# Up projection: eight column pairs with two feature blocks by seven products instead of four, and their quarters loaded by GpSimd

## The chip, the core and the metric

The kernel runs on one core of a Trainium2 chip. A core has a matrix engine (TensorE, PE in the profile; its weight loads are PEld), three engines for other arithmetic (VectorE or DVE, ScalarE or ACT, GpSimd or POOL), and SyncE (SP), which here only issues loads and stores. Each engine runs its own list of instructions in order and waits for others by semaphores. Loads move between the chip's memory and the core's SBUF; TensorE writes into PSUM, eight banks of 128 x 512 float32. The metric is the device time in microseconds, lower is better. Three runs of the kernel before gave a median of 1549.39 us (1548.16 to 1551.18).

## The reference

One decoder layer over 256 tokens of width 2048, all in float32: a norm, a combined input projection, two parallel token mixers, an output projection, a residual sum, then the part that matters here and a final norm:

```python
h = rmsnorm(x, norm_ffn_w[l])
gate, up = jnp.split(jnp.einsum('bsd,df->bsf', h, w_up[l]), 2, axis=-1)
gate = causal_dwconv(gate, conv_ffn_w[l]) + conv_ffn_b[l]
x = x + jnp.einsum('bsf,fd->bsd', jax.nn.gelu(gate, approximate=False) * up, w_down[l])
```

The up projection multiplies the 256 x 2048 activations by a 2048 x 11264 weight matrix: 5632 gate columns and 5632 up columns.

## The kernel before

**Precision and tiles.** Weights come as tiles of 256 x 512 (`raw`, 512 KB a load). ScalarE rounds a tile to float32r (`whi`, L278), VectorE subtracts that from the tile (`wlo`, L286), and a product is three matmuls: high by high, low activation by high weight, high activation by low weight. `whi` and `wlo` have three buffers each and `raw` four; `weights()` makes tiles two ahead of the one in use.

**Stages.** Input projection and mixers come first, then the output projection (L321 to L323, from `w_out`), the up projection (L1353, 819 to 1303 us of the span), and the down projection (L1338).

**The up projection** goes by 11 column pairs c = 0 to 10, each 512 gate columns and the 512 up columns that belong to them. The 2048 features are four blocks of 512. A block is either done plainly, by four steps `("plain", c, col, kp)` of 12 matmuls (two 256-feature halves by gate and up; `up_plain`), or as a 2 x 2 block product by seven products instead of eight (Strassen and Winograd's form): feature halves j, token halves t, gate and up as the two columns. `chunks_of[c]` says which blocks go by seven: none in pair 0, block 0 in every other pair, and blocks 1 and 0 in the pairs of `TWO`, (1, 3, 5, 7).

**The seven products** (`up_product`, L1356 and on) are T1, 11, T2, 21, T3, 22, T4, with 6 matmuls each. 11, 21 and 22 use one quarter of the weights as it is, and T1 to T4 use sums of quarters, which `up_sum` (L219) makes on VectorE in place: four a block. Four quarters of a block are loaded by `quad_load` (L213) with SyncE into homes (`UP_HOMES`), buffers that hold something else earlier or later: xt0 to xt3 for block 0, hhi8 to hlo9 for block 1. The activations' sums (`ups`) are made once, in pair 0, for blocks 0 and 1 alike.

**Banks.** T1 opens an own bank (from the pool `psm`, two buffers, which the transposed gate and up use as well) and ends in a copy to SBUF (L1382). 11 opens the bank of gate and second token half; behind the last block's 11, ScalarE copies that bank to the gate's other token half (L1386), and T2, T3 and T4 go on adding into the first one. Before the first 21 and behind the last T3, VectorE adds the own bank to make the two banks of up (L1375, L1389).

**The order around them** is written out by hand in `up_steps` and fixed for TensorE. With g a plain gate step, u a plain up step of pair c, and p a product of pair c + 1, the last up steps of c (`rest`) are put between the first products of c + 1. Before a pair of `TWO` six up steps are kept back (`tail`): T1, u, 11, u (block 1), T1, u, 11, u (block 0), T2, u (block 1), T2, u (block 0), then 21 twice, the transposes of pair c's gate (L1415), T3 twice, 22 twice, the transposes of its up, T4 twice. The gate's convolution (L1305, L1310), gelu, and the product with up follow during the next plain steps. `when` says how many steps ahead of its place each quarter's load is written. The order on ScalarE, VectorE, GpSimd and the queues is a scheduler's, made when the program is built.

**GpSimd** before loads only the down projection's quarters (L232) and some small things; the second norm's power (L560) runs on it at 824.63 us.

Of the kernel before, what the change touches and what calls it, by code (L numbers as in the profile page):

```python
# [8 lines left out]
F32 = mybir.dt.float32  # L9
# [5 lines left out]
P = 128  # L15
# [20 lines left out]
def kernel(  # L36
# [20 lines left out]
    nc = tc.nc  # L57
# [11 lines left out]
    def nm(s):  # L69
        cnt[0] += 1  # L70
        return f"{s}_{cnt[0]}"
# [5 lines left out]
    def cols(w, base, nk):  # L77
        return [w[c * 256 : (c + 1) * 256, base : base + 512].rearrange("(k p) f -> p k f", p=P)
                for c in range(nk // 2)]
# [13 lines left out]

    srcs += outw[0][:6] + outw[1][:6] + outw[0][6:] + outw[1][6:] + outw[2] + outw[3]
    NUP = DFF // 512
    TWO = (1, 3, 5, 7)
    chunks_of = [()] + [(1, 0) if c in TWO else (0,) for c in range(1, NUP)]
    UP_PARTS = ("T1", "11", "T2", "21", "T3", "22", "T4")
    up_w = [(cols(w_up[0], 512 * c, KD), cols(w_up[0], DFF + 512 * c, KD)) for c in range(NUP)]
    up_steps = []  # L100
    TAIL = 3
    for c in range(NUP):
        kps = [kp for kp in range(KD // 2) if kp // 2 not in chunks_of[c]]
        gate_steps, up_only = ([("plain", c, col, kp) for kp in kps] for col in range(2))
        tail = 6 if c + 1 in TWO else TAIL
        up_steps += gate_steps[:tail]
        for a, b in zip(gate_steps[tail:], up_only):
            up_steps += [a, b]
        rest = up_only[-tail:]
        if c + 1 == NUP:  # L110
            up_steps += rest
            break
        parts = [[("part", c + 1, what, ch) for what in UP_PARTS] for ch in chunks_of[c + 1]]
        up_steps += [("loads", c + 1)]
        if c + 1 in TWO:
            first_four = [parts[ch][n] for ch in range(2) for n in (0, 1)] + [parts[ch][2] for ch in range(2)]
            for a, b in zip(first_four, rest):
                up_steps += [a, b]
            p21, t3, p22, t4 = ([parts[ch][n] for ch in range(2)] for n in range(3, 7))
            up_steps += p21 + [("gate", c)] + t3 + p22 + [("up", c)] + t4  # L120
        else:
            t1, p11, t2, p21, t3, p22, t4 = parts[0]
            up_steps += [t1, rest[0], p11, rest[1], t2, rest[2], p21, ("gate", c), t3, p22, ("up", c), t4]
# [5 lines left out]
    sums_behind = {}  # L129
    for n, src in enumerate(srcs):  # L130
        if isinstance(src, tuple):
            what, ch = src[2:]
            if src[1] not in TWO:
                behind = {"T1": [(n, "T2", 0)], "T2": [(n, "T3", 0), (n, "T4", 0)]}.get(what, [])
            else:
                behind = {("11", 1): [(n, "T1", 0), (n + 1, "T2", 1)], ("T1", 0): [(n + 1, "T2", 0)],
                          ("T2", 1): [(n, "T3", 1), (n + 1, "T4", 1)],
                          ("T2", 0): [(n, "T3", 0), (n + 1, "T4", 0)]}.get((what, ch), [])
            for at_, sum_, of in behind:
                sums_behind.setdefault(at_, []).append((sum_, of))  # L140
    down = [cols(w_down[0], 512 * c, KF) for c in range(4)]

    SEVEN = (8, 9, 10)
# [36 lines left out]
    made = []  # L180
# [3 lines left out]
    last_load = [None]  # L184
# [19 lines left out]
    up_quarters = {}  # L204
    UP_BUFFER = {"11": 0, "T1": 1, "T2": 1, "T3": 0, "21": 2, "22": 3, "T4": 1}

    UP_HOMES = (("xt0", "xt1", "xt2", "xt3"), ("hhi8", "hlo8", "hhi9", "hlo9"))

    def quad_load(c, n):

        ch, i = n // 4, (1, 0, 3, 2)[n % 4]
        up_quarters[ch, i] = fp.tile([P, 2, 512], F32, tag=UP_HOMES[ch][i], name=nm("quad"))
        last_load[0] = nc.sync.dma_start(up_quarters[ch, i], up_w[c][i % 2][2 * ch + i // 2]).ins  # L213

    def up_sum(what, ch):
        b11, b12, b21, b22 = (up_quarters.get((ch, i)) for i in range(4))
        for out_, plus_, minus_ in {"T1": [(b12, b12, b11)], "T2": [(b12, b22, b12)],
                                    "T3": [(b11, b12, b11)], "T4": [(b12, b21, b12)]}[what]:
            nc.vector.tensor_tensor(out_, plus_, minus_, op=ALU.subtract)  # L219
# [15 lines left out]
    def quarter(half, chunk, what, ch=0):  # L235

        if half == "up":
            return up_quarters[ch, UP_BUFFER[what]]
        b11, b12, b21, b22 = (quarters.get((half, chunk, w)) for w in ("11", "12", "21", "22"))
        sums = {"T1": (b11, b12, b11), "T3": (b12, b22, b12), "T2": (b22, b22, b11), "T4": (b21, b21, b22)}  # L240
        return sums[what] if what in sums else quarters[half, chunk, what]
# [24 lines left out]
    def begin(n):  # L266
        while len(made) < min(len(srcs), n):
            load(len(made) + 1)
            raw = loads[len(made)]
            if isinstance(raw, tuple):  # L270
                raw, plus, minus = raw
                nc.vector.tensor_tensor(raw, plus, minus, op=ALU.subtract)
            src = srcs[len(made)]
            shape = list(raw.shape)
            keep = kept.get(len(made))
            hi = wpool.tile(shape, F32R, tag="whi", name=nm("whi")) if keep is None else \
                mtile(keep, shape, F32R, nm("khi"))
            nc.scalar.copy(hi, raw)  # L278
            if shape[1] == 8:
                lo = None  # L280
                nc.vector.tensor_tensor(hi[:, :, 32:64], raw[:, :, 0:32], hi[:, :, 0:32].bitcast(F32),
                                        op=ALU.subtract)
            else:
                lo = wpool.tile(shape, F32R, tag="wlo", name=nm("wlo")) if keep is None else \
                    mtile(4 + keep, shape, F32R, nm("klo"))
                last_split[0] = nc.vector.tensor_tensor(lo, raw, hi.bitcast(F32), op=ALU.subtract).ins  # L286
                splits.append(last_split[0])
            made.append((hi, lo))
            for what, ch in sums_behind.get(len(made) - 1, ()):
                up_sum(what, ch)  # L290
            if isinstance(src, tuple) and src[0] != "up" and src[2] in ("T1", "T3", "T2", "T4"):
                next_quarter()

# [93 lines left out]
    def mtile(i, shape, dt, name):  # L387
        return big.tile(shape, dt, tag=f"m{i}", name=name)
# [280 lines left out]
    tail = mp.tile([P, NH], F32, name="tail")  # L669
# [538 lines left out]
    fp = ctx.enter_context(tc.tile_pool(name="ffn", bufs=1))  # L1208
# [217 lines left out]
    for i, step in enumerate(up_steps):  # L1426
        if step[0] == "part":
            up_product(*step[1:])
            if step[2] == "T4" and step[3] == chunks_of[step[1]][-1]:
                def elementwise(c=step[1] - 1, gates=gates, ups=ups):  # L1430
                    yield from gate_part(c, gates)
                    up_part(c, ups)
                    yield

                work[:] = [elementwise()]
        elif step[0] == "gate":
            gates = turned_pair(pending[step[1], 0])
        elif step[0] == "up":
            ups = turned_pair(pending[step[1], 1])
        elif step[0] == "plain":  # L1440
            up_plain(*step[1:])
            if step[1:] == (0, 0, 1):
                turned_rows()
            if step[1] == 0 and step[2] == 0 and step[3] in (3, 5):
                up_ups.append(up_sums(len(up_ups)))
            if step[1] == NUP - 1 and step[2] == 0:
                if step[3] == 5:
                    half_sums(SEVEN[0])
                if 4 <= step[3]:
                    next_quarter()  # L1450
            if work:
                next(work[0], None)
        for n, step in enumerate(up_steps):
            if step[0] == "loads":
                when = (6, 5, 4, 3, 12, 11, 10, 9) if step[1] in TWO else (8, 7, 6, 5)
                for q in sorted(range(len(when)), key=lambda q: -when[q]):
                    if max(n - when[q], 0) == i:
                        quad_load(step[1], q)
                if n - 3 == i:
                    up_sum("T1", chunks_of[step[1]][0])  # L1460
    pe_order.close()

    xts = {}
# [32 lines left out]
    for hf in range(2):  # L1496
# [11 lines left out]
        for n, step in enumerate(steps[hf]):  # L1508
# [9 lines left out]
            if step[0] == "plain":  # L1518
                kp, c = step[1], step[2] % 2
                more = any(x[0] == "plain" and x[2] % 2 == c for x in steps[hf][n + 1 :]) or hf == 1  # L1520
# [4 lines left out]
            chunk, what = step[1:]  # L1525
# [128 lines left out]
```

## Time and profile before

| | us |
|---|---|
| median of three runs | 1549.39 |
| the profiled execution | 1548.64 |
| its span, first to last instruction | 1546.8 |
| TensorE busy | 1533.0 |
| VectorE busy | 1227.4 |
| ScalarE busy | 842.9 |
| GpSimd busy | 65.6 |

A line of a group names the source line, the engine, the operation, what it writes and reads, its shape and its count; behind the bar stand the busy time, the mean of one in ns, and the engine's idle time just before, with what ended it. A line of a window gives its length, then the busy time and count of each engine, the granted clock, the DMA engines' busy share and GB/s. A line of the chain gives start, length and what ran. A line of the timeline gives start, length and the instruction, with its engine's idle time in brackets where it waited. A line of waits gives who waited for whom, the total, the count and the longest.

### The profile page before, as it was taken

The page shows a single profiled execution, that of the slowest core. Times are in us where ns is not written, and L with a number is a line of the kernel's source. Part 1 is how long each engine was busy: PE and PEld are TensorE (multiplying, and loading weights), DVE is VectorE, ACT ScalarE, POOL GpSimd, SP SyncE. Part 2 cuts the span into 40 slices and gives each one's busy share as a digit, 9 for nine tenths or more (in the row PEclk, how much of TensorE's full clock was granted, in tenths as well). Part 3 has the DMA queues.
Part 4 walks back from the last instruction along what each step waited for, and adds up shares of the span by engine and source line. Part 5 has one row for each costly group of instructions (what it writes and reads, how often), then busy time and mean ns, then how long its engine had stood idle before and what let it go on. Part 6 is the DMA issues. An engine that isn't in the chain of part 4 may idle for free.

```text
span 1546.8 us, 20166 instructions
## 1 busy us (share of the span) xinstructions
PE 1533.0 (99%) x7326; PEld 1264.2 (82%) x7326; DVE 1227.4 (79%) x1748; ACT 842.9 (54%) x1051; POOL 65.6 (4%) x82
## 2 busy tenths in 40 slices
PE   9999999999999999999999999999999999999998
PEld 8888888788888888888877888888888888788886
DVE  6688858896689858887585898888888876878885
ACT  6455446454545445454454666666666665545552
POOL 1010002000100000000000000000000000000100
PEclk9999999999999999999999999999999999999999
DMA  8776757776577756675686565757656667556652
GB/s 276 210 224 206 202 155 224 210 215 181 166 236 210 199 168 200 215 211 183 211 305 191 180 206 163 218 171 220 178 175 192 190 199 256 189 186 204 222 191 90
DMA packets 167698, 310.46 MB, mean 201 GB/s; under 512 B 19459, under 2 KB 23331, under 8 KB 167471
## 3 DMA queue, kind: packets, MB, share of 16 engines
q1 hardware_dynamic: 159456, 287.37, 60.9%
q0 software_dynamic: 4032, 14.68, 2.9%
q10 hardware_dynamic: 4110, 7.13, 1.3%
q8 instruction: 57, 0.93, 0.3%
q14 instruction: 43, 0.34, 0.1%
HBM read 301.75 MB, written 7.38 MB: 200 GB/s over the span
## 4 chain that ended last, share of the span: by engine, by line
PE 96%; DMA 2%; issue 1%; DVE 1%; ACT 0%; POOL 0%; POOLq 0%; SPq 0%; DVEq 0%
PE psg L1353 29%; PE psm L323 15%; PE psm L321 14%; PE psm L322 14%; PE psm L1338 7%; PE psg L1338 7%; PE psm L467 1%; PE psm L1353 1%; PE psm L1415 1%; PE psg L366 1%; PE psg L857 1%; DMA raw<-in_w_out_dram 1%; DMA quad<-in_w_up_dram 0%; PE psg L859 0%; DVE wlo L286 0%
## 5 line engine op out<-in xcount | busy, mean ns | idle before, releaser
L278 ACT CAST whi<-raw 128x1024 fp32r<-128x1024 f32 x444 | 467.8, 1055 | 440.1 <-PE psm L322 270.9
L286 DVE TENSOR_TENSOR wlo<-raw,whi 128x1024 fp32r<-128x1024 f32 x442 | 538.4, 1222 | 145.8 <-ACT whi L278 138.0
L286 DVE TENSOR_TENSOR wlo<-quad,whi 128x1024 fp32r<-128x1024 f32 x140 | 171.2, 1224 | 59.7 <-ACT whi L278 58.0
L278 ACT CAST whi<-quad 128x1024 fp32r<-128x1024 f32 x140 | 147.8, 1056 | 120.5 <-PE psg L1353 67.8
L323 PE MATMUL psm<-wlo,xhl 128*128 128x512 f32 x432 | 169.5, 393 | 0.6 <-DVE wlo L286 0.6
L321 PE MATMUL psm<-whi,xhl 128*128 128x512 f32 x432 | 169.0, 391 | 0.0
L322 PE MATMUL psm<-whi,xhl 128*128 128x512 f32 x432 | 168.6, 390 | 0.0
L1353 PE MATMUL psg<-whi,fhl 128*128 128x512 f32 x504 | 127.4, 390 | 0.0
L1353 PEld LDWEIGHTS psg<-whi,fhl 128*128 128x128 f32 x504 | 94.2, 188 | 19.2
L323 PEld LDWEIGHTS psm<-wlo,xhl 128*128 128x128 f32 x432 | 81.1, 188 | 17.8 <-DVE wlo L286 1.2
L322 PEld LDWEIGHTS psm<-whi,xhl 128*128 128x128 f32 x432 | 81.1, 188 | 16.9
L321 PEld LDWEIGHTS psm<-whi,xhl 128*128 128x128 f32 x432 | 81.1, 188 | 16.7
L219 DVE TENSOR_TENSOR quad<-quad,quad 128x1024 f32<-128x1024 f32 x56 | 68.5, 1223 | 11.0 <-DMA quad<-in_w_up_dram 6.0
L1353 PE MATMUL psg<-wlo,fhl 128*128 128x512 f32 x252 | 69.9, 389 | 0.0
L1338 PE MATMUL psm<-wlo,hhi 128*128 128x512 f32 (+1 forms) x150 | 58.1, 387 | 0.5 <-DVE wlo L286 0.5
L1338 PE MATMUL psm<-whi,hhi 128*128 128x512 f32 (+1 forms) x150 | 58.2, 388 | 0.2 <-ACT whi L278 0.2
L1338 PE MATMUL psm<-whi,hlo 128*128 128x512 f32 (+1 forms) x150 | 57.9, 386 | 0.0
L1353 PEld LDWEIGHTS psg<-wlo,fhl 128*128 128x128 f32 x252 | 47.3, 188 | 9.8
L321 PE MATMUL psm<-whi,mhi 128*128 128x512 f32 x128 | 51.0, 398 | 0.5 <-ACT whi L278 0.5
L323 PE MATMUL psm<-wlo,mhi 128*128 128x512 f32 x128 | 50.3, 393 | 0.5 <-DVE wlo L286 0.5
L1338 PE MATMUL psg<-whi,hhi 128*128 128x512 f32 (+1 forms) x130 | 50.3, 387 | 0.2 <-ACT whi L278 0.2
L1338 PE MATMUL psg<-whi,hlo 128*128 128x512 f32 (+1 forms) x130 | 50.0, 386 | 0.0
(430 smaller groups left out, 2942.9 us busy)
## 6 DMA issues: line engine op xcount, KB each, us to landing
raw<-in_w_in_dram SPq DMA_DIRECT2D x224, 512.0 KB, 4.4
raw<-in_w_up_dram SPq DMA_DIRECT2D x120, 512.0 KB, 4.3
raw<-in_w_down_dram SPq DMA_DIRECT2D x64, 512.0 KB, 4.7
quad<-in_w_up_dram SPq DMA_DIRECT2D x56, 512.0 KB, 4.6
raw<-in_w_out_dram SPq DMA_DIRECT2D x32, 512.0 KB, 4.6
quad<-in_w_down_dram POOLq DMA_DIRECT2D x24, 512.0 KB, 5.2
mv<-vrow SPq DMA_DIRECT2D x12, 512.0 KB, 4.8
taps<-in_conv_qkv_w_dram SPq DMA_DIRECT2D x16, 256.0 KB, 6.5
```

The source lines that it names most:

```text
L219: nc.vector.tensor_tensor(out_, plus_, minus_, op=ALU.subtract)
L278: nc.scalar.copy(hi, raw)
L286: last_split[0] = nc.vector.tensor_tensor(lo, raw, hi.bitcast(F32), op=ALU.subtract).ins
L321: mm(ps[:, t, :], lh(k, t), hi[:, kk, :], start=(k == 0), stop=False)
L322: mm(ps[:, t, :], ll(k, t), hi[:, kk, :], start=False, stop=False)
L323: mm(ps[:, t, :], lh(k, t), lo[:, kk, :], start=False, stop=(k == nk - 1))
L366: nc.tensor.transpose(pt[:, ff, t * P : (t + 1) * P], src[:, t, f * P : (f + 1) * P], ident)
L467: mm(ps_k0[:, t, :], part(k, t), w[:, kk, :], start=(k == 0 and w is hi and part is xh), stop=(k == KD - 1 and w is lo))
L857: mm(pg0, kq[:, h, 0, 0:P], kq[:, h, :, :], start=True, stop=True)
L1338: mm(ps[:, cs], lhs(kk), part_[:, kk, cs], start=(first and kk == 0 and n == 0), stop=(last and kk == 1 and n == 2), skip_group_check=shared)
L1353: mm(ps, lhs(kk), w[n][:, kk], start=(first and n == 0 and kk == 0 and lhs is high), stop=False, skip_group_check=True)
L1415: nc.tensor.transpose(out_[f // 2][:, f % 2, t * P : (t + 1) * P], e[:, t, f * P : (f + 1) * P], ident)
```

## The change

`TWO` becomes (1, 2, 3, 4, 5, 6, 7, 9), so that blocks 1 and 0 go by seven products in eight pairs. Pairs 2 to 7 now follow a pair that itself has two such blocks and so only four gate and four up steps: all four up steps are kept back, and the list sets one behind each of the first three products and one behind block 1's T2, with none behind block 0's 11 and T2. The homes alternate between two sets by odd and even pairs (block 1: hhi8 to hlo9, and hhi6 to hlo7; block 0: xt0 to xt3 in two orders), the quarters are kept by pair as well, the loads are issued by GpSimd (L216 after), and `when` for a pair of two blocks changes. The source lines behind it move by three: L1353 is L1356 after, L1386 is L1389, L1310 is L1313, L286 is L289.

```diff
-    TWO = (1, 3, 5, 7)
+    TWO = (1, 2, 3, 4, 5, 6, 7, 9)
...
-        tail = 6 if c + 1 in TWO else TAIL
+        tail = min(6, len(kps)) if c + 1 in TWO else TAIL
...
+            if len(rest) == 4:
+                rest = rest[:3] + [None] + rest[3:] + [None]
             for a, b in zip(first_four, rest):
-                up_steps += [a, b]
+                up_steps += [a, b] if b else [a]
...
-                sums_behind.setdefault(at_, []).append((sum_, of))
+                sums_behind.setdefault(at_, []).append((src[1], sum_, of))
...
-    UP_HOMES = (("xt0", "xt1", "xt2", "xt3"), ("hhi8", "hlo8", "hhi9", "hlo9"))
+    UP_HOMES = ((("xt0", "xt1", "xt2", "xt3"), ("hhi8", "hlo8", "hhi9", "hlo9")),
+                (("xt0", "xt2", "xt1", "xt3"), ("hhi6", "hlo6", "hhi7", "hlo7")))
...
-        up_quarters[ch, i] = fp.tile([P, 2, 512], F32, tag=UP_HOMES[ch][i], name=nm("quad"))
-        last_load[0] = nc.sync.dma_start(up_quarters[ch, i], up_w[c][i % 2][2 * ch + i // 2]).ins
+        up_quarters[c, ch, i] = fp.tile([P, 2, 512], F32, tag=UP_HOMES[1 - c % 2][ch][i], name=nm("quad"))
+        nc.gpsimd.dma_start(up_quarters[c, ch, i], up_w[c][i % 2][2 * ch + i // 2])
...
-    def up_sum(what, ch):
-        b11, b12, b21, b22 = (up_quarters.get((ch, i)) for i in range(4))
+    def up_sum(c, what, ch):
+        b11, b12, b21, b22 = (up_quarters.get((c, ch, i)) for i in range(4))
...
-            return up_quarters[ch, UP_BUFFER[what]]
+            return up_quarters[chunk, ch, UP_BUFFER[what]]
...
-                when = (6, 5, 4, 3, 12, 11, 10, 9) if step[1] in TWO else (8, 7, 6, 5)
+                when = (7, 7, 6, 5, 13, 12, 11, 10) if step[1] in TWO else (8, 7, 6, 5)
...
-                    up_sum("T1", chunks_of[step[1]][0])
+                    up_sum(step[1], "T1", chunks_of[step[1]][0])
```

More of the change, by code (lines that the diff above doesn't have):

```diff
@@ L288, in begin @@
             made.append((hi, lo))
-            for what, ch in sums_behind.get(len(made) - 1, ()):
-                up_sum(what, ch)
+            for more in sums_behind.get(len(made) - 1, ()):
+                up_sum(*more)
             if isinstance(src, tuple) and src[0] != "up" and src[2] in ("T1", "T3", "T2", "T4"):
```

## The prediction

> **What bounds the kernel now.** I read the page first, then TensorE's waits, then one period of the up projection by windows, by groups and by chain, and last its timeline around one product.
>
> ```profile
> span 1546.8 us, 20166 instructions
> PE 1533.0 (99%) x7326; PEld 1264.2 (82%) x7326; DVE 1227.4 (79%) x1748; ACT 842.9 (54%) x1051; POOL 65.6 (4%) x82
> PE 96%; DMA 2%; issue 1%; DVE 1%; ACT 0%; POOL 0%; POOLq 0%; SPq 0%; DVEq 0%
> PE psm L1235 <- DVE fhl L1241: 2.5, 1, 2.5
> PE psm L323 <- DVE wlo L286: 1.1, 2, 0.6
> PE psm L321 <- ACT whi L278: 0.5, 1, 0.5
> 879.13:965.83 86.70, 86.70 (x400) 72.06 (x399) 75.81 (x80) 58.30 (x67) 0.00 (x0) 1.00 0.63 194
> 920.93 17.69 PE psg L1353 x78
> 938.62 1.36 PE psm L1353 x6
> ```
>
> TensorE is 96% of the chain, and the list of its waits has nothing from the up projection (L1353): 2.5 us stand at its beginning, 1.6 in the output projection. The window is one period of two column pairs there, one with two feature blocks by seven products and one with one: TensorE 86.70 of 86.70 us, VectorE 75.81, ScalarE 58.30, the granted clock 1.00. The chain gives the price of a matmul: 17.69 / 78 = 0.227 us. A product has 6 (1.36 us), a plain step 12 (2.72 us). So a matmul less is worth 0.227 us, as long as nobody comes later than TensorE.
>
> **The change part by part.** *Matmuls.* In four more pairs (2, 4, 6, 9) feature block 1 goes by seven products of 6 instead of four plain steps of 12: 42 for 48. 4 x 6 = 24 matmuls x 0.227 = 5.4 us less, all on the path. Both built programs show these 24, so that the change does what it says is no question.
>
> *VectorE and ScalarE.* Each of the four new blocks has three more tiles to split and four sums of quarters.
>
> ```profile
> L286 DVE TENSOR_TENSOR wlo<-quad,whi 128x1024 fp32r<-128x1024 f32 x22 | 26.8, 1224 | 6.2 <-ACT whi L278 6.0
> L219 DVE TENSOR_TENSOR quad<-quad,quad 128x1024 f32<-128x1024 f32 x12 | 14.7, 1223 | 2.0 <-issue 1.0 <-DMA quad<-in_w_up_dram 0.9
> 970.88 1.22 DVE L286 TENSOR_TENSOR wlo<-quad,whi 128x1024 fp32r<-128x1024 f32 x1
> 972.01 0.48 DVE L1310 SCALAR_TENSOR_TENSOR y<-psm,cfw,y 128x254 f32<-128x254 f32 x1
> 972.40 1.22 DVE L286 TENSOR_TENSOR wlo<-quad,whi 128x1024 fp32r<-128x1024 f32 x1
> 973.53 1.22 DVE L286 TENSOR_TENSOR wlo<-raw,whi 128x1024 fp32r<-128x1024 f32 x1
> ```
>
> A row lasts 1.22 us, but the starts show that a split costs 1.13 us of VectorE in a run of them, a step of the gate's convolution 0.39. Seven more make 75.81 + 7 x 1.13 = 83.7 us in a period that is to last 86.70 - 1.36 = 85.3. It fits, at 98% by this upper count, so I cost it at nothing; but its cover, the 11 us that VectorE was idle, is nearly gone. ScalarE has three casts of 1.06 us more: 61.5 of 85.3.
>
> *The order of a pair that follows a pair of two blocks* (pairs 2 to 7, six times). It has four up steps left to put between the first products, not six. The new list sets none behind 11 of block 0: T2 of block 1 follows at once. Behind 11 stands a copy of its bank (L1386), and T2 goes on adding into the bank that is copied, so TensorE must wait for the copy; the built program has this wait. ScalarE's built order has one cast ahead of the copy. Before, the same three rows lie so:
>
> ```profile
> 950.70 1.07 PE L1353 MATMUL psg<-whi,fhl 128*128 128x512 f32 x4
> 951.60 0.61 PE L1353 MATMUL psg<-wlo,fhl 128*128 128x512 f32 x2
> 951.80 1.06 ACT L278 CAST whi<-raw 128x1024 fp32r<-128x1024 f32 x1 [0.76 <-PE psg L1353]
> 952.06 1.98 PE L1353 MATMUL psg<-whi,fhl2b 128*128 128x512 f32 x8
> 952.76 0.58 ACT L1386 COPY psg<-psg 128x512 f32<-128x512 f32 x1
> 954.78 1.07 PE L1353 MATMUL psg<-whi,ups 128*128 128x512 f32 x4
> 779.28 0.50 PE L321 MATMUL psm<-whi,mhi 128*128 128x512 f32 x1 [0.54 <-ACT whi L278]
> 779.61 0.40 PE L322 MATMUL psm<-whi,mlo 128*128 128x512 f32 x1
> ```
>
> Product 11 runs from 950.70 to 952.06. The cast needs the weight buffer that 11's high half frees, starts 0.20 us behind that, at 951.80, and the copy follows and ends at 953.34. Before, an up step (952.06 to 954.78) hides it, and T2 starts at 954.78. Without that step T2 could start at 952.06 and stands until 953.34: 1.28 us. A restart costs 0.04 for the signal and 0.10 in its first matmul (779.28 to 779.61 is 0.33, not 0.23). 1.42 us, six times: 8.5 us. The least, with no cast ahead, is 0.20 + 0.58 + 0.14 = 0.92 (5.5 in all); I take 8.5, since the cast does stand ahead and can't start earlier. Behind the waiting T2, all of TensorE stands.
>
> *The own bank.* T1 opens a bank in the buffer that the previous pair's transposed gate leaves, and so waits for the last convolution step on that gate. Now four plain steps lie between, not five or six.
>
> ```profile
> 972.16 0.88 PE psm L1415 x8
> 973.04 16.33 PE psg L1353 x72
> 989.37 1.36 PE psm L1353 x6
> 987.20 0.48 DVE L1310 SCALAR_TENSOR_TENSOR y<-psm,cfw,y 128x254 f32<-128x254 f32 x1
> ```
>
> Here T1 comes after two products and five plain steps, at 989.37, and the last convolution step is done at 987.68. One step of 2.72 earlier, T1 would start at 986.65 and wait 1.03 us. That is the upper end; the lower is nothing, since the new VectorE order draws the convolution steps forward. That order, from T4's split at 970.88 on, has 11 splits and sums and 7 convolution steps up to there: 11 x 1.13 + 7 x 0.39 = 15.2 us, to 986.0, only 0.6 before 986.65. I take 0.15, near the lower end, six times: 0.9 us.
>
> *Quarters by GpSimd.* 72 loads of up weights go to GpSimd's queue (56 were quarters on SyncE's, 16 plain).
>
> ```profile
> L213 SPq DMA_DIRECT2D quad<-in_w_up_dram x56: 367/368/932, 759.3 to 1222.4; - x56
> DMA to landing us min/median/max: 3.6/4.6/13.4
> L232 POOL DMA_DIRECT2D quad<-in_w_down_dram x24: 724/724/909, 1261.1 to 1469.9; - x24
> DMA to landing us min/median/max: 4.3/5.2/8.7
> 965.23 2.48 DVE L286 TENSOR_TENSOR wlo<-quad,whi 128x1024 fp32r<-128x1024 f32 x2
> ```
>
> A landing there takes 5.2 us against 4.6. The bytes stay the same. The tightest load is block 0's 11: its home is free when T3's split is done (966.46, the first of the two at 965.23), and its sum T1 now stands in VectorE's order ahead of the last T4 split. TensorE needs that split ten matmuls behind 973.04, at 975.3, so the sum (1.13), a convolution step (0.39) and the split (1.22) must begin by 972.6: 6.1 us after the home came free. I cost it at nothing for a landing of 5.2; one of 8.7 costs 2.6 us in that pair. SyncE loses 72 issues of 0.37 us, and no plain load queues behind a quarter any more; nothing waited for that in the up projection, so the gain is nothing. GpSimd's power for the second norm now stands behind three quarters that are free long before it: nothing.
>
> *The first loads.* Eight quarters instead of four start at once in the output projection.
>
> ```profile
> 765.00:770.00 5.00, 5.00 (x24) 4.14 (x23) 3.26 (x3) 1.36 (x2) 0.00 (x0) 1.00 1.05 397
> 775.00:780.00 5.00, 4.46 (x23) 3.15 (x21) 4.55 (x10) 3.18 (x8) 0.00 (x0) 1.00 1.05 393
> ```
>
> DMA is full there, and TensorE lost 0.5 + 0.5 us at 779 and 780 to late plain tiles, which stood behind quarters in one queue. Two more megabytes at 395 GB/s are 5.3 us. Ends: -1.1 (that loss goes, as the queues part) and +5.3 (all of it delays plain tiles). I take 0, since both act.
>
> *Sum:* -5.4 + 8.5 + 0.9 + 0 + 0 = +4.0 us. The profiled execution took 1548.64 us (span 1546.8 and 1.8 around it), so 1552.6; it lay 0.75 below the median of 1549.39, and against that 1553.4 us. All lower ends together give -5.4 + 5.5 - 1.1 = -1.0, all upper ones without late loads -5.4 + 8.5 + 6.2 + 5.3 = +14.6.
>
> [...]
>
> **The rivals.** *Faster: the copy is hidden.* If T2 doesn't in fact find the copy outstanding, because TensorE already stands for something shorter ahead of 11 (a late split), the 8.5 us shrink below 2.3 and the saved matmuls show: with -1.1 from the first loads, 1549.4 - 5.4 - 1.1 = 1543 at best. It decides below 0.4 us per copy. For it: no wait of this kind is in the trace of before. Against it: the rows above, where the copy ends 1.28 us behind its product.
>
> *Slower by more: VectorE and late quarters bound.* At 98% VectorE has no room for a load that lands late: with 1.03 us at each own bank, and landings of 6.7 us (0.6 over the 6.1), it is 6 x (1.03 + 0.6) = 9.8 instead of 0.9, so 1562. For it: landings up to 8.7. Against it: the copy's stall gives VectorE 1.4 us a pair to catch up.
>
> *Even: the short copy.* At 0.92 us per copy and nothing else, 5.5 - 5.4: 1549.5.
>
> **How the numbers follow.** A measurement of this kernel can tell about 0.2%, 3.1 us, from no change. The forecast has 0.66 (its own range 1551 to 1557; a quarter of it lies within 0.2%), the faster rival 0.08, the bound VectorE 0.16, the short copy 0.10. Slower: 0.50 + 0.16 = 0.66; same: 0.16 + 0.10 = 0.26; faster 0.08. The range leaves out the faster rival and the far part of the slower: 1548 to 1560.
>
> **What would show it.** Six waits of TensorE for ScalarE's copy, near 1.4 us each, right behind product 11; TensorE's busy time or its count 24 matmuls lower; a period of the up projection of about 88 us where it was 86.7; waits of T1 for the gate's convolution of 0.2 us or less; GpSimd's loads landing in 5 to 6 us. Wrong if the waits for the copy are under 0.5 us, if the period is under 86 us, or if TensorE waits for splits in the middle of a pair.

## The result and the profile after

The changed kernel took 1559.86 us (median of four, 1559.28 to 1561.91), beside 1548.95 for the kernel before: a ratio of 1.0070, 95% interval 1.0058 to 1.0082. It is slower, by 10.9 us where 4.0 were forecast; the time lies 0.14 us inside the range (1548 to 1560). The profiled execution has a span of 1557.6 us, 10.8 more than before.

From the page of the changed kernel: span, busy times, and the chain's shares by engine. Behind it, TensorE's waits (who waited for whom, total, count, longest).

```profile
span 1557.6 us, 20232 instructions
...
PE 1531.2 (98%) x7302; PEld 1259.3 (81%) x7302; DVE 1257.9 (81%) x1776; ACT 851.5 (55%) x1063; POOL 117.2 (8%) x154
...
PE 91%; DMA 4%; issue 3%; DVE 2%; ACT 1%; POOL 0%; POOLq 0%; SPq 0%; DVEq 0%
```

```profile
PE psg L1356 <- ACT psg L1389: 7.0, 6, 1.2
PE psm L326 <- DVE wlo L289: 3.3, 4, 1.6
PE psm L1238 <- DVE fhl L1244: 2.5, 1, 2.5
PE psm L324 <- ACT whi L281: 2.4, 1, 2.4
...
PE psg L1356 <- DVE psg L1392: 0.6, 1, 0.6
```

The 24 matmuls are gone (7302 for 7326), and the six forecast waits for ScalarE's copy are there. But the chain has DMA at 4% where it had 2, and two waits of 2.4 and 1.6 us stand in the output projection (L324, L326), for a cast and a split of plain tiles. The same stretches of both kernels by windows (length, then busy time and count of PE, PEld, DVE, ACT, POOL, the granted clock, DMA share, GB/s): 300 matmuls up to the first one of the up projection, the up projection, and the rest. Before:

```profile
753.18:819.33 66.15, 65.08 (x301) 53.40 (x300) 48.56 (x66) 34.58 (x51) 0.34 (x1) 1.00 0.84 290
819.33:1302.97 483.64, 481.17 (x2197) 399.48 (x2196) 397.50 (x415) 307.26 (x351) 6.68 (x9) 1.00 0.64 195
1302.97:1546.80 243.83, 235.25 (x1061) 193.81 (x1059) 187.30 (x193) 122.44 (x134) 15.62 (x22) 0.99 0.54 181
```

After, and two windows within its output projection:

```profile
753.60:825.95 72.35, 67.99 (x301) 55.40 (x300) 50.27 (x67) 34.82 (x51) 8.45 (x12) 0.95 0.84 294
825.95:1314.56 488.61, 477.94 (x2174) 392.82 (x2173) 426.00 (x442) 316.60 (x363) 50.60 (x70) 1.00 0.60 189
1314.56:1557.60 243.04, 234.68 (x1061) 194.09 (x1059) 187.25 (x193) 122.24 (x134) 15.58 (x22) 0.99 0.54 181
...
785.00:790.00 5.00, 1.09 (x4) 0.30 (x2) 4.93 (x9) 2.09 (x2) 0.72 (x1) 0.90 1.05 401
790.00:795.00 5.00, 4.96 (x12) 3.94 (x13) 3.55 (x3) 2.80 (x3) 0.72 (x1) 0.50 0.87 304
```

So the 10.8 us are +0.4 ahead of the window, +6.2 in the output projection, +5.0 in the up projection and -0.8 in the rest. The up projection's share is near the forecast. The output projection's was costed at nothing.

**The output projection.** The chain of the changed kernel there (start, length, what ran):

```profile
764.14 18.68 DMA quad<-in_w_up_dram
...
782.91 1.23 DVE quad L222
...
788.77 1.23 DVE wlo L289
790.04 0.80 PE psm L326
790.84 0.43 PE psm L324
```

GpSimd issued eight quarters in one go from 760.4 us on, since all their homes were free: pair 1's block 1 and, about 135 us before their use, pair 2's. One of the latter took 18.7 us to land on a DMA that moved 400 GB/s. Its sum (L222) stood early in VectorE's order, in front of nearly 5 us of small work and of the split that TensorE needed (the wait of 1.6 us). VectorE itself stood only 0.21 us for that landing, as the first row below shows, so what the sum took from the split is mainly its own 1.2 us. The wait of 2.4 us just before ended with a cast, which the timeline shows released by a plain tile's transfer:

```profile
782.91 1.23 DVE L222 TENSOR_TENSOR quad<-quad,quad 128x1024 f32<-128x1024 f32 x1 [0.21 <-DMA quad<-in_w_up_dram]
...
786.64 1.04 ACT L281 CAST whi<-raw 128x1024 fp32r<-128x1024 f32 x1 [3.52 <-DMA raw<-in_w_out_dram]
```

So TensorE idled twice within 6 us and then ran 12 matmuls at a granted clock of 0.50: the chain's 0.43 us instead of 0.227. The three waits there (a third of 0.4 us stands at 782.8) are 4.86 us beyond the normal pace, from start to start, where before had 1.41. The clock adds 12 x 0.2 = 2.40, and 0.36 in the matmul just ahead of these twelve. 4.86 - 1.41 + 2.40 + 0.36 = 6.2.

**The copy.** The timeline of the changed kernel around one of the six waits:

```profile
916.77 1.06 ACT L281 CAST whi<-raw 128x1024 fp32r<-128x1024 f32 x1 [0.73 <-PE psg L1356]
918.38 0.61 PE L1356 MATMUL psg<-wlo,fhl 128*128 128x512 f32 x2
918.58 1.05 ACT L281 CAST whi<-quad 128x1024 fp32r<-128x1024 f32 x1 [0.76 <-PE psg L1356]
919.54 0.58 ACT L1389 COPY psg<-psg 128x512 f32<-128x512 f32 x1
920.17 1.20 PE L1356 MATMUL psg<-whi,ups 128*128 128x512 f32 x4 [1.17 <-ACT psg L1389]
```

Product 11's last matmul starts at 918.61, T2's first at 920.17: 1.56 us instead of 0.227, six times, 8.0 us. T2's second matmul follows 0.34 us behind its first, so the restart adds 0.11 each time. The cast stands ahead of the copy, as forecast.

### The profile page after: what moved, and what is told of

Its sections match the earlier page's. It is cut to its first block, busy times and chain, and to the rows that moved or that the text cites. A ratio compares the mean times of both kernels' runs of the same rounds, so it can differ in the third digit from the quotient of the medians.

```text
span 1557.6 us, 20232 instructions
## 1 busy us (share of the span) xinstructions
PE 1531.2 (98%) x7302; PEld 1259.3 (81%) x7302; DVE 1257.9 (81%) x1776; ACT 851.5 (55%) x1063; POOL 117.2 (8%) x154
## 4 chain that ended last, share of the span: by engine, by line
PE 91%; DMA 4%; issue 3%; DVE 2%; ACT 1%; POOL 0%; POOLq 0%; SPq 0%; DVEq 0%
PE psg L1356 26%; PE psm L326 14%; PE psm L324 14%; PE psm L325 14%; PE psm L1341 7%; PE psg L1341 7%; DMA quad<-in_w_up_dram 2%; PE psm L1356 2%; PE psm L470 1%; PE psm L1418 1%; PE psg L369 1%; DMA vrow<-ev 1%; PE psg L860 1%; DVE wlo L289 1%; DMA mv<-vrow 1%
## 5 line engine op out<-in xcount | busy, mean ns | idle before, releaser
L281 ACT CAST whi<-raw 128x1024 fp32r<-128x1024 f32 x428 | 450.1, 1052 | 444.1 <-PE psm L325 281.9
L289 DVE TENSOR_TENSOR wlo<-raw,whi 128x1024 fp32r<-128x1024 f32 x426 | 517.5, 1220 | 148.8 <-ACT whi L281 143.3
L281 ACT CAST whi<-quad 128x1024 fp32r<-128x1024 f32 x168 | 177.0, 1054 | 132.7 <-PE psg L1356 75.3
L289 DVE TENSOR_TENSOR wlo<-quad,whi 128x1024 fp32r<-128x1024 f32 x168 | 204.8, 1222 | 50.4 <-ACT whi L281 48.3
L326 PE MATMUL psm<-wlo,xhl 128*128 128x512 f32 x432 | 169.6, 393 | 1.3 <-DVE wlo L289 1.3
L324 PE MATMUL psm<-whi,xhl 128*128 128x512 f32 x432 | 169.1, 392 | 0.0
L1356 PE MATMUL psg<-whi,fhl 128*128 128x512 f32 x504 | 127.4, 390 | 0.6 <-DVE psg L1392 0.6
L1356 PEld LDWEIGHTS psg<-whi,fhl 128*128 128x128 f32 x504 | 94.5, 188 | 20.5 <-ACT whi L281 0.8
L326 PEld LDWEIGHTS psm<-wlo,xhl 128*128 128x128 f32 x432 | 81.1, 188 | 18.7 <-DVE wlo L289 2.1
L324 PEld LDWEIGHTS psm<-whi,xhl 128*128 128x128 f32 x432 | 81.2, 188 | 16.6
L222 DVE TENSOR_TENSOR quad<-quad,quad 128x1024 f32<-128x1024 f32 x72 | 87.4, 1220 | 3.6 <-DMA quad<-in_w_up_dram 2.5
L216 POOL DMA_DIRECT2D quad<-in_w_up_dram x72 | 52.2, 726 | 421.9 <-DVE wlo L289 366.8
L1356 PE MATMUL psg<-wlo,fhl 128*128 128x512 f32 x252 | 70.0, 390 | 0.0
L1356 PE MATMUL psg<-whi,ups 128*128 128x512 f32 x216 | 59.8, 398 | 7.0 <-ACT psg L1389 7.0
L1356 PEld LDWEIGHTS psg<-wlo,fhl 128*128 128x128 f32 x252 | 47.2, 188 | 10.3 <-DVE wlo L289 0.5
L324 PE MATMUL psm<-whi,mhi 128*128 128x512 f32 x128 | 52.0, 407 | 2.4 <-ACT whi L281 2.4
L326 PE MATMUL psm<-wlo,mhi 128*128 128x512 f32 x128 | 51.5, 403 | 2.0 <-DVE wlo L289 2.0
```

The lines of the kernel that those rows point to most:

```text
L216: nc.gpsimd.dma_start(up_quarters[c, ch, i], up_w[c][i % 2][2 * ch + i // 2])
L324: mm(ps[:, t, :], lh(k, t), hi[:, kk, :], start=(k == 0), stop=False)
L326: mm(ps[:, t, :], lh(k, t), lo[:, kk, :], start=False, stop=(k == nk - 1))
L1356: mm(ps, lhs(kk), w[n][:, kk], start=(first and n == 0 and kk == 0 and lhs is high), stop=False, skip_group_check=True)
```

## The experiments

Times are medians; each ratio, with its 95% interval, is to runs of the kernel before on the same chip.

### Pair 2's first loads later

```diff
+        with ExitStack() as behind:
+            for other in pair_1 if c == 2 else ():
+                behind.enter_context(tc.issue_after(other))
-        nc.gpsimd.dma_start(up_quarters[c, ch, i], ...)
+            load = nc.gpsimd.dma_start(up_quarters[c, ch, i], ...)
+        if c == 1:
+            pair_1.append(load.ins)
...
+            with tc.issue_after(last_split[0]) if (c, what, ch) == (2, "T1", 1) else ExitStack():
                 nc.vector.tensor_tensor(out_, plus_, minus_, op=ALU.subtract)
```

> The changed kernel with one part undone: GpSimd issues pair 2's eight quarters only behind pair 1's last one (issued at 836 us in the changed kernel, in the up projection, instead of 763 us), and VectorE makes pair 2's first sum where the program has it. My theory: of the 10.9 us lost, 6.6 were lost in the output projection (TensorE waits of 0.4, 2.4 and 1.6 us, then 5 us at half the granted clock), because pair 2's four quarters were loaded there 120 us before their use. Then the first matmul of the up projection comes at 819 to 820 us again, not 826, no granted clock below 0.9 stands before it, and the time is 1559.9 - 6.6 = 1553.3 (ratio to the kernel before 1.003). Rival, the queue: GpSimd's queue by itself, with pair 1's four quarters alone in it, delays the plain tiles; then at least 3 us of the 6.6 stay and the time is 1556.5 or more. Rival, the loss only moves: 2 MB that land at 836 us delay the plain tiles there, waits of 3 to 6 us appear behind 836 and the time stays at 1557 to 1560.

1559.05 us, 1.0055 (1.0043 to 1.0068): hardly faster. Its two stretches by windows, and its waits (L1364 is this kernel's up product):

```profile
755.13:820.15 65.02, 64.70 (x301) 53.48 (x300) 48.54 (x66) 34.55 (x51) 5.58 (x8) 1.00 0.84 294
820.15:1314.56 494.41, 480.97 (x2174) 395.06 (x2172) 427.82 (x443) 317.17 (x363) 53.47 (x74) 0.99 0.61 191
```

```profile
PE psg L1364 <- ACT psg L1397: 7.0, 6, 1.2
...
PE psm L1364 <- DVE y L1321: 2.4, 1, 2.4
```

The output projection did what the theory said: 65.02 us, 7.3 less, with the clock at 1.00. But the time didn't follow, since the up projection is 5.8 longer. Of these, 1.6 are slow matmuls behind the second norm, which the changed kernel's profiled execution didn't have (last section); most of the rest comes from my edit. It had put pair 2's first sum where the program has it, in a stretch in which VectorE was busy without a break. That pushed the gate's last convolution step (`y`, L1321) back, and T1's own bank waited 2.4 us for it, with seven matmuls at half the clock behind it. That is the place and mechanism of the prediction's slower rival, brought about here by the edit.

### Only the sum later, the loads as early as in the changed kernel

The last two lines of the diff above, alone.

> The changed kernel, with the eight first quarters loaded as early as it does, but with VectorE's first sum for pair 2 kept back to its place in the program (two pairs later) instead of standing in front of the splits of the output projection's plain tiles. It parts two causes of the 6.6 us lost there. If VectorE stood behind the landing of a quarter (the sum at 782.9 us waits for a quarter issued at 764.1), the waits at 783 and 790 us go, the clock is not reduced to half, and the time falls by 4 or more, to 1556 or less. If the plain tiles themselves were late, because 2 MB more were on a DMA that moved 400 GB/s already, the wait of 2.4 us at 785 us stays, and the time falls by under 2, to 1558 or more.

1561.86 us, 1.0081 (1.0067 to 1.0095).

```profile
754.37:824.60 70.23, 67.16 (x302) 54.39 (x301) 49.15 (x66) 34.88 (x51) 8.46 (x12) 0.98 0.87 303
824.60:1317.07 492.47, 479.45 (x2174) 393.72 (x2173) 427.85 (x443) 316.88 (x363) 50.59 (x70) 1.00 0.60 187
```

The total is spoiled by the same new wait of 2.4 us at 900 us. It stands here although the quarters come early, so the sum's place causes it and not the moved loads. The output projection's window decides the question. With VectorE free of the sum, 70.23 us: 2.1 less than 72.35, and 5.2 more than with the loads later (65.02). So most of the loss there is the 2 MB themselves, which hold up the plain tiles' transfers, and 2.1 us is the sum's place in VectorE's order (one profiled execution each). Both numbers contain slow matmuls: about 1.6 of the 5.2 and 1.2 of the 2.1.

### A plain step behind block 0's 11

```diff
-                rest = rest[:3] + [None] + rest[3:] + [None]
+                rest = rest + [None, None]
```

> The changed kernel with the last plain up step of six pairs moved from behind T2 of block 1 to behind 11 of block 0, so that it stands again between the copied bank and the product that adds into it. My theory: the six waits for ScalarE's copy (start to start 1.56 us instead of 0.227, 8.0 us in all) go, and the time is 1559.9 - 8.0 = 1551.9. Rival, VectorE: T2, T2, 21, 21 now follow each other without a plain step, 5.4 us of TensorE for four splits and two sums of 1.13 (6.8 us); with its buffers empty VectorE is late by up to 1.4 us in each of the six pairs, and the waits only change their releaser: 1557 to 1560.

1553.20 us, 1.0026 (1.0015 to 1.0036): 6.7 us less than the changed kernel.

```profile
825.22:1306.63 481.41, 476.61 (x2174) 392.98 (x2173) 424.27 (x442) 317.39 (x363) 50.59 (x70) 1.00 0.61 192
```

```profile
PE psg L1356 <- DVE wlo L289: 0.8, 2, 0.6
...
PE psm L1356 <- ACT whi L281: 0.3, 1, 0.3
```

The up projection lost 7.2 us (488.61 to 481.41). None of TensorE's waits names the copy any more; the two rows are what came in its place, 1.1 us. So the copy's wait was the cause, and VectorE's rival is small: T2, T2, 21, 21 in a row don't empty its buffers for long.

### Both edits

> Both edits together (pair 2's quarters and first sum later, the plain step behind 11 of block 0). If the two losses are separate and additive, the time is 1559.9 - 6.6 - 8.0 = 1545.3, that is 0.998 of the kernel before: 24 matmuls less (5.4 us) minus about 2 us of own-bank and late-sum waits that stay. If VectorE's margin is the real bound of the new pairs, one wait takes the place of the other and the time is 1550 or more.

1551.15 us, 1.0011 (1.0002 to 1.0020). Not additive: the wait at 900 us came back, 3.28 us from start to start, with seven slow matmuls.

```profile
903.19 0.47 PE L1364 MATMUL psm<-whi,ups 128*128 128x512 f32 x1 [2.89 <-DVE y L1321]
```

### The sum in VectorE's slack

To the kernel with both edits:

```diff
-            with tc.issue_after(last_split[0]) if (c, what, ch) == (2, "T1", 1) else ExitStack():
+            with tc.issue_after(splits[-16]) if (c, what, ch) == (2, "T1", 1) else ExitStack():
```

> The run with both edits, but with VectorE's first sum for pair 2 behind the split of sixteen tiles earlier, among pair 0's plain steps (at about 860 us), where VectorE is busy 30 of 40 us, and not in the full stretch at 900 us. With the sum kept back to its place in the program, TensorE waited 3.28 us (start to start) at 899.9 us for T1 of pair 2 and then ran seven matmuls at half the granted clock (0.43 instead of 0.227 us). My theory: that wait comes from the late sum alone; it goes, with 3.0 us, and with it the half clock, 1.4 us: 1551.2 - 4.4 = 1546.8, 0.998 of the kernel before. Rival: VectorE is short of time in pair 2 whatever the order, because the loads are later; then a wait of 2 us or more stands at 895 to 905 us again and the time is 1550 or more.

1547.04 us, 0.9991 (0.9983 to 1.0000). T1's wait at 900 us is 0.5 from start to start, without a slow matmul behind it. 4.1 us less for the place of one VectorE instruction of 1.2 us: the loss at 900 us in the runs above was the sum's place, and not a shortage of VectorE's time. A quarter can still come late: in this execution a later sum stood 1.96 us for its quarter, and the split behind it kept TensorE waiting 1.5 us at 932.6 us.

### Pair 9's sum as well

```diff
+            behind = {(2, "T1", 1): splits[-16], (9, "T1", 0): last_sum[0]}.get((c, what, ch))
+            with tc.issue_after(behind) if behind else ExitStack():
```

> As the run with the sum in VectorE's slack, and besides the first sum of block 0 of pair 9 stands behind pair 8's second bank sum on VectorE, not ahead of it. In the changed kernel and in the runs so far TensorE waits 0.9 to 1.4 us there (start to start), since the bank sum stands behind a sum that waits for a quarter issued 5.2 us before. My theory: that wait goes, 0.7 to 1.2 us, and the time is 1.0 less than of the run beside it, 1545.8. Rival: the split of pair 9's first tiles is late instead, and the time is the same.

1546.55 us, 0.9985 (0.9976 to 0.9994): this version beats both kernels, by 2.4 us the one before. From its page, its waits, and its two stretches by windows (L1365 is the up product):

```profile
span 1543.5 us, 20236 instructions
...
PE 96%; DVE 1%; DMA 1%; issue 1%; ACT 0%; POOLq 0%; POOL 0%; SPq 0%; DVEq 0%
```

```profile
PE psm L335 <- DVE wlo L298: 1.8, 2, 1.0
PE psg L1365 <- DVE wlo L298: 1.2, 3, 0.7
```

```profile
753.66:819.22 65.56, 64.71 (x302) 53.54 (x300) 48.62 (x66) 34.56 (x51) 5.60 (x8) 1.00 0.83 291
819.22:1300.18 480.96, 476.71 (x2174) 392.87 (x2172) 424.72 (x443) 317.13 (x363) 53.59 (x74) 1.00 0.62 197
```

Pair 9's wait is gone from the list; the timed gain over the run beside it, 0.5 us, is within their scatter. The up projection is 2.7 us shorter than before, and 1.6 of these are slow matmuls behind the second norm that this execution happened not to have (last section). So about 1.1 of the 5.4 us that 24 matmuls are worth arrives. Three waits for splits (1.7 us beyond the normal pace, from start to start) and five waits of T1 (1.4, at 0.5 from start to start) are most of the rest.

### GpSimd alone

The kernel before, with one line changed:

```diff
-        last_load[0] = nc.sync.dma_start(up_quarters[ch, i], ...).ins
+        nc.gpsimd.dma_start(up_quarters[ch, i], ...)
```

> The kernel before with one part of the change alone: its quarters are issued by GpSimd instead of SyncE; four pairs with two blocks, the old homes and the old order. The prediction costs this part at nothing in the up projection, and in the first loads its lower end was -1.1 (TensorE's two waits of 0.5 us at 779 and 780 us go, as plain tiles no longer stand behind quarters in one queue). My theory: the time stays within 1549 +- 1.5. [...]

1547.26 us, 0.9995 (0.9986 to 1.0004): no difference. The windows, and the landing of its 56 quarters:

```profile
756.15:821.34 65.19, 64.74 (x302) 53.54 (x300) 48.62 (x66) 34.56 (x51) 5.59 (x8) 1.00 0.84 293
821.34:1304.89 483.55, 481.08 (x2198) 399.31 (x2197) 397.76 (x415) 306.37 (x351) 42.02 (x58) 1.00 0.63 195
...
L213 POOL DMA_DIRECT2D quad<-in_w_up_dram x56: 724/724/909, 762.9 to 1224.6; - x56
...
DMA to landing us min/median/max: 4.0/5.1/14.7
```

The up projection is as long as before (483.55 and 483.64), the output projection 1.0 us shorter (65.19 and 66.15): the queues part, as the prediction's lower end had it.

### The copy ahead of the casts

The changed kernel, with ScalarE's copy issued ahead of two casts in six pairs (`c in (2, 3, 4, 5, 6, 7)`):

```diff
-        w = weights()
+        w = weights(AHEAD - 1 if what == "11" and ends_ and c in (2, 3, 4, 5, 6, 7) else AHEAD)
...
+                copies.append(last_copy[0])
...
+            with tc.issue_after(copies.pop()) if copies else ExitStack():
                 nc.scalar.copy(hi, raw)
```

> The changed kernel with one order of ScalarE turned round: in the six pairs that follow a pair of two blocks, the copy of block 0's bank stands ahead of the casts of the next plain step and of T2 of block 0, and not behind them. It prices the cast inside the six waits. The prediction's lower end for such a wait was 0.92 us with no cast ahead of the copy, against 1.42; measured were 1.33 with the cast ahead. My theory: the six waits shrink by 0.5 each, to about 0.85, and the time to 1559.9 - 3.0 = 1556.9. Rival: the casts that now stand behind the copy are late in their turn, the next plain step waits for its split, and the time stays at 1559 to 1560.

1558.50 us, 1.0059 (1.0047 to 1.0072). One wait by the timeline, and the up projection by windows:

```profile
919.05 0.61 PE L1358 MATMUL psg<-wlo,fhl 128*128 128x512 f32 x2
919.70 0.57 ACT L1391 COPY psg<-psg 128x512 f32<-128x512 f32 x1 [2.99 <-PE psg L1358]
920.19 1.05 ACT L283 CAST whi<-raw 128x1024 fp32r<-128x1024 f32 x1
920.33 0.96 PE L1358 MATMUL psg<-whi,ups 128*128 128x512 f32 x3 [0.66 <-ACT psg L1391]
```

```profile
826.45:1313.28 486.83, 478.12 (x2174) 392.43 (x2173) 423.81 (x442) 315.68 (x363) 50.60 (x70) 1.00 0.60 189
```

Each wait is 1.05 us from start to start instead of 1.56, so the cast's share of it is 0.51, as expected; over six, 3.1 us. The up projection is only 1.8 shorter, since other waits grew by 1.3 (pair 9's from 0.86 to 1.49 from start to start), and of the timed 1.4 us the intervals can't tell how much is real.

### The best version with SyncE's queue

```diff
-            load = nc.gpsimd.dma_start(up_quarters[c, ch, i], ...)
+            load = nc.sync.dma_start(up_quarters[c, ch, i], ...)
```

> The version with both edits and both sums in their new places, its 72 quarters issued by SyncE instead of GpSimd, as in the kernel before. In the kernel before, the same exchange alone made no measurable difference (0.9995 of it). Theory: none here either, 1546.6 +- 1.5. Rival: with eight quarters in a pair SyncE's one queue matters, since a quarter that waits for its home holds up the plain tiles issued behind it; then waits for casts and splits of plain tiles appear in the up projection and the time is 1550 or more.

1548.92 us, 0.9999 (0.9990 to 1.0008), between the two expectations. The up projection took 484.45 us against 480.96. Of these 3.5 us, 1.4 are slow matmuls behind the second norm, which this execution had and the other not. The rest has waits of T1 for the gate's last convolution step up to 0.8 us, and one of 0.9 that the profile puts down to ScalarE, though it too ends 0.15 us behind that step. The landing is 4.9 us by either queue. In the output projection TensorE's two waits at 779 and 781 us are back (0.95 and 0.92 from start to start), as in the kernel before. By the intervals the 0.14% between the two versions are likely but not certain.

## Why the prediction was right, and where its size came from

The time lies in the range, but by 0.14 us, and outside the 1551 to 1557 of the main forecast; the change is 10.9 us and not 4.0. That the range still held it is luck: its upper part was meant for other causes. The terms of the up projection are right in cause and nearly in size, and a term costed at nothing brought the excess.

**Matmuls**, -5.4: right, by the count of 24.

**The copy**, +8.5: right in place, cause and number of waits; measured +8.0, 1.33 each beyond the normal pace. The forecast's 1.42 counts the restart as well; with it the wait is 1.33 + 0.11 = 1.44, or +8.7. The plain step behind 11 took the wait away, and the copy put first showed the cast's part of it, 0.51. The lower end, 0.92 without the cast, was measured as 1.05 - 0.23 + 0.11 = 0.93.

**The own bank**, +0.9: five waits of 0.27, +1.4. Right in kind, since each of the five ends 0.15 us behind the last convolution step; a little above the 0.2 us that the prediction named as a sign. Its upper end was read too low: the chain, from which it took T1's start (989.37), has that start 0.17 us later than the timeline (989.20), so it was 1.2 us and not 1.03. For the same reason the room for the tightest load was 5.9 us and not 6.1, which a landing of 5.0 still meets. The new order did draw the convolution steps forward, as far as VectorE's order allowed. The runs with pair 2's sum moved show what the upper end stood for: a sum more in front of the last step, and T1 waits 2.4 us.

**VectorE**, nothing: right in the period. The window of two pairs has it at 83.45 us, where 83.7 was the count, and no split was late inside a pair:

```profile
884.12:973.18 89.06, 86.50 (x395) 70.60 (x393) 83.45 (x87) 60.86 (x70) 11.28 (x16) 1.00 0.59 187
```

The period is 89.06 us, not about 88: two copies and two own banks. The nothing is shown for this order alone: with a plain step behind 11 and the copy's waits gone, splits come late in three of four versions with GpSimd's queue (0.8, 1.5 and 1.2 us of waits; none with both edits). Whether the copy's waits gave VectorE the time, as the prediction argued against its slower rival, is not shown.

**Quarters by GpSimd**, nothing: right. Issued by GpSimd alone, the quarters cost no measurable time (0.9995, 0.9986 to 1.0004), with a median landing of 5.1 us where SyncE's, before, had 4.6.

**The first loads**, nothing between -1.1 and +5.3: this is the term that was mis-sized. It measured +6.2 us. The prediction took 0 between two ends, "since both act". Both do, but they aren't of one size: the parted queues gave -1.0 (GpSimd alone), the 2 MB +5.2 (sum later against loads later). What it had not seen is the sum's place: the scheduler had put pair 2's first sum in front of the output projection's splits, 2.1 us. Part of these sums is a price that the prediction did not have at all, the half clock behind a long wait, 2.8 us of the 6.2. So the match of the 5.2 with the 5.3 of the upper end is in part luck, since about 1.6 of it is the clock. The trace of before showed both sides: a DMA already at a busy share of 1.05, and matmuls at half the clock behind its one wait of 2.5 us.

**The rivals.** The copy was neither hidden nor short (1.33 us each), and VectorE was late for no split in the up projection of the changed kernel. None of the rivals is where the excess came from.

The rest, +0.6 for pair 9's late sum, -1.6 for slow matmuls that the changed kernel happened not to have behind its second norm, +1.3 in small intervals of the up projection, +0.4 ahead of the output projection, and -0.8 behind the up projection, was in no term.

## What to carry to other kernels

When a buffer gets a second set of homes, ask when its first load can start: a home that is free early starts its transfer early, and on the full DMA here a transfer for later delayed those of now. Look as well at where a scheduler puts a long operation in the list of an in-order engine: one sum of 1.2 us cost 2.1 us in front of the output projection's splits, about 4 in a full stretch of VectorE, and its T1 waited no longer than the others' when it stood among plain steps. Pair 2's loads and the sums of pairs 2 and 9 in new places turned +10.9 us into -2.4, together with a step moved between a copied bank and the next product into it. Price a long wait of TensorE with the slow matmuls behind it: here they were 2.8 of the 6.2 us lost in the output projection.

## What was unexpected in the hardware

The granted clock was halved behind some waits of TensorE and not behind others of the same length. The same wait of 2.5 us for the second norm stands in both kernels and in seven experiments' lists of waits. Before, then after, by windows around it:

```profile
826.00:828.00 2.00, 0.15 (x1) 0.15 (x2) 1.25 (x3) 0.47 (x1) 0.00 (x0) 1.00 0.73 251
828.00:830.00 2.00, 2.00 (x9) 1.67 (x9) 0.48 (x1) 0.90 (x2) 0.00 (x0) 0.65 0.92 267
830.00:832.00 2.00, 2.00 (x7) 1.52 (x6) 0.48 (x1) 0.28 (x2) 0.00 (x0) 0.50 0.75 237
```

```profile
832.00:834.00 2.00, 0.00 (x1) 0.00 (x0) 1.46 (x3) 0.95 (x2) 0.00 (x0) 1.00 0.94 290
834.00:836.50 2.50, 2.03 (x11) 1.78 (x12) 0.90 (x2) 0.78 (x2) 0.74 (x1) 1.00 0.77 229
```

Before, the granted clock was 0.50 from 828.62 to 832.03 us, and the matmuls there took 0.43 us each, 1.6 us more in all. The changed kernel had no slow matmul behind this wait; its clock was 0.50 from 788.98 to 795.80 us, in the output projection. Of the experiments, those with pair 2's loads later (1.6 us) and with SyncE's queue (1.4 us) had slow matmuls behind the norm's wait, and those with both edits (1.00 from 820 to 840 us) and with both sums moved (0.999 over the whole execution) had none.

Behind the waits of 2.4 us and more for T1 at 900 us the matmuls were slow in all three executions that had one. With pair 2's loads later the granted clock was 0.58 from 903.2 to 907 us, and with both edits 0.50 from 905 to 907 us. With only the sum later, TensorE was busy for 479.45 us in the up projection, beside 477.94 in the changed kernel, with the same count of matmuls. Behind the changed kernel's six waits of 1.2 us for the copy the clock stayed at 1.00.

So the same wait cost 1.6 us in one execution and nothing in another. What decides between the two is not shown here.
